# Low weight parts of three plain pairs of the MLP made by a negated copy and an adding DMA

## The chip, the cores and the metric

The kernel runs on one core of a Trainium2 chip. The metric is the device time of one execution in microseconds (us), here the median of several. The core has five engines that run beside each other and wait for each other by semaphores: TensorE (PE in the profile, with its weight loads as PEld), VectorE (DVE), ScalarE (ACT), GpSimd (POOL) and SyncE (SP). SP computes nothing here; it issues the DMA transfers that bring weights from the chip's main memory.

## The reference: two layers of a hybrid decoder

Activations are 256 x 2048 in float32, and there are two layers. A layer computes

- `proj = rms_norm(x) @ w_in`, whose columns feed eight heads of gated linear attention and eight heads of stick-breaking attention;
- `x = x + mixed @ w_o`, with the normalised outputs of both groups in `mixed`;
- `up = square(relu(rms_norm(x) @ w_up))` with 8192 columns, and `x = x + up @ w_down`.

The two matrices of the MLP (2048 x 8192 and 8192 x 2048) hold most of the weights. Each weight is used once per layer, for all 256 tokens.

## The kernel before

**Products in two parts.** TensorE multiplies at its fast rate in a rounded type, fp32r. To keep float32 accuracy the kernel splits each operand in a high part (the value rounded to fp32r) and a low part (the value minus its high part), and replaces a product by three: high by high, high by low, low by high. For a weight tile, ScalarE makes the high part `whi` with a rounding copy (L984) and VectorE the low part `wlo` with a subtraction (L988). This is `parts`.

**Units and pairs.** The listed stage of a layer (`listed`) is a list of units. A unit multiplies an operand by 1024 columns of weights. In the MLP there are four quarters q, and each holds four units: `up` with n2 = 0 and 1, then `down` with n2 = 0 and 1. Over both layers that makes 16 up units and 16 down units. A unit runs over eight pairs j = 0 to 7; a pair is two blocks of 128 rows of weights, loaded by one SP transfer of 1 MB into a tile `raw` (128 partitions x 2 rows k x 1024 columns). There are four such raw tiles. The transfer for pair x waits in SP's queue until every reader of pair x - 4 is done.

**Plain and fast pairs.** Some pairs are computed by a scheme that saves a product by sums of blocks (`FAST`: pairs 1, 2, 4, 5 of an up unit and 1, 4, 5 of a down unit); VectorE forms these sums of weights (L821) before the parts are made. A fast pair has four pieces of parts, with 2, 1, 2 and 2 products. The other pairs are plain: two pieces, one for each half of 512 columns c, each holding both rows k. A product is the three matmuls of `product` (L1078), each 128 x 128 by 512 columns. A plain piece feeds two banks of the accumulator, banks 2 and 4 for c = 0 and banks 3 and 8 for c = 1, with the products of both rows k in each, so it is 12 matmuls.

**The ring.** The parts live in a ring of five slots (`RING`). Piece i may be written only when the matmuls of piece i - 5 are done, which leaves four pieces of matmuls as its lead.

**Banks and seeds.** In a down unit each of banks 2, 4, 3 and 8 starts from the residual: ScalarE copies `xt` into it (`seeds`, L1100) before its first matmul. It can do so only when VectorE has taken the sums of the unit before out of that bank (`finals`, L821). In an up unit the first matmul clears the bank, and only the `finals` of the unit before have to be done. At the start of a unit that follows an up unit, TensorE also transposes that unit's result (L1233), after the first and after the second piece.

**Order.** `Plan` sets the order of all this. Each piece of work has an engine, a planned length and a lag. TensorE's and SP's orders are as written; a due time is worked out backwards for the others, and a simulated run gives ScalarE and VectorE, whenever one is free, the ready piece that is due first. The instructions are then written out in that order, engine by engine, and each engine runs its own list in order. In this stage GpSimd has a few memsets, in the units before the MLP.

Of the kernel before, what the change touches and what calls it, by code (L numbers as in the profile page):

```python
# [11 lines left out]
F32R = mybir.dt.float32r  # L12
BF16 = mybir.dt.bfloat16
AF = mybir.ActivationFunctionType
ALU = mybir.AluOpType
AX = mybir.AxisListType

P = 128
# [21 lines left out]
class Plan:  # L40
# [20 lines left out]
    def add(self, engine, length, fn, *deps, lag=0.0):  # L61
        flat = []
        for d in deps:
            flat.extend(d if isinstance(d, (list, tuple)) else [d])
        self.pieces.append(Plan.Piece(engine, length, fn, [d for d in flat if d], lag))
        return self.pieces[-1]

    def run(self):
        t = 0.0
        for p in self.pieces:  # L70
            if p.engine == "PE":
                p.due = t
                t += p.length
        begins = {"DVE": t, "ACT": t}
        unset = {p: len(p.users) for p in self.pieces if p.engine != "PE"}
        last = []

        def settled(p):
            for d in p.deps:
                if d in unset:  # L80
                    unset[d] -= 1
                    if not unset[d]:
                        push(d)

        def push(p):
            end = min([u.due for u in p.users], default=t) - p.lag - self.GAP
            heapq.heappush(last, (-end, -at_of[p], p))

        at_of = {p: i for i, p in enumerate(self.pieces)}
        for p in self.pieces:  # L90
            if p in unset and not p.users:
                push(p)
        for p in reversed(self.pieces):
            if p.engine == "PE":
                settled(p)
        while last:
            end, _, p = heapq.heappop(last)
            p.due = min(-end, begins.get(p.engine, t)) - p.length
            if p.engine in begins:
                begins[p.engine] = p.due  # L100
            settled(p)
        line = {e: [p for p in self.pieces if p.engine == e] for e in ("PE", "SP")}
        free = dict.fromkeys(("PE", "SP", "DVE", "ACT"), 0.0)
        left = {p: len(p.deps) for p in self.pieces}
        at = dict.fromkeys(self.pieces, 0.0)
        ready = {"DVE": [], "ACT": []}
        order, events, count = [], [], 0
        for p in self.pieces:
            if not p.deps:
                events.append((0.0, count, p))  # L110
                count += 1
        came = set()
        while events:
            now, _, p = heapq.heappop(events)
            if p is not None:
                if p.engine in ready:
                    heapq.heappush(ready[p.engine], (p.due, count, p))
                else:
                    came.add(p)
                count += 1  # L120
            for e in free:
                if free[e] > now + 1e-9:
                    continue
                if e in ready:
                    if not ready[e]:
                        continue
                    p = heapq.heappop(ready[e])[2]
                elif line[e] and line[e][0] in came:
                    p = line[e].pop(0)
                else:  # L130
                    continue
                order.append(p)
                free[e] = now + p.length
                heapq.heappush(events, (free[e], count, None))
                count += 1
                for u in p.users:
                    at[u] = max(
                        at[u], free[e] + p.lag + (0.0 if u.engine == e else self.GAP)
                    )
                    left[u] -= 1  # L140
                    if not left[u]:
                        heapq.heappush(events, (at[u], count, u))
                        count += 1
        assert len(order) == len(self.pieces)
        for p in order:
            if p.fn:
                p.fn()
        return max(free.values())
# [3 lines left out]
def trunk_kernel(  # L152
# [17 lines left out]
    nc = tc.nc  # L170
# [51 lines left out]

    ATT = ("v4", "tri", "nones", "ident16", "wg", "reset", "mask16", "lr", "lrT", "ha", "hh", "hl", "hA", "on", "row", "bc")
    MLP = (*(f"{t}{i}" for t in ("whi", "wlo") for i in range(4, 12)), "sxh1", "sxk", "sx1", "sx2", "ts", "t4", "raw2")
    MANUAL = {mybir.EngineType.SP, mybir.EngineType.PE, mybir.EngineType.DVE, mybir.EngineType.Activation}

    def tmp(tag, shape, dt=F32, bufs=2):
        pool = pools["att"] if tag in ATT else pools["mlp"] if tag in MLP else tpool
        return pool.tile(list(shape), dt, tag=tag, name=nm(tag), bufs=bufs)
# [7 lines left out]
    def f32(ap):  # L237
        return ap.bitcast(F32)
# [173 lines left out]
            return self.t[k // 2][:, k % 2].rearrange("p a t -> p (a t)")  # L412

    FAST = {"up": (1, 2, 4, 5), "down": (1, 4, 5)}
    KEPT = 4
    HEAD_KINDS = ("sk", "sv", "gv")
    QUICK = (
# [158 lines left out]
    def part_tile(tag, turn, shape):  # L576
        slot = f"{tag}{turn % 4}"
        return ppool.tile(shape, F32R, tag=slot, name=nm(tag), bufs=1)
# [229 lines left out]
    def listed(l, front, mixed=None, old=None, linear=None):  # L808
# [7 lines left out]
        add = plan.add  # L816
        MM, TR, V2, V1, A2, A1 = 0.227, 0.108, 1.15, 0.61, 1.0, 0.55
        RING, RAWS = 5, 4
# [30 lines left out]
        free = {}  # L849
        whi, wlo, raws = [], [], []  # L850
        part_base = part_turn[0] % 4
        up, done = {}, {}
# [119 lines left out]
        def parts(src, readers, deps, n=2):  # L972
# [23 lines left out]
            readers.extend((h, lo))  # L996
            return box, h, lo

        last = {}
        sums13, sums4 = [], []  # L1000


        def steps(u, j, is_fast, r, ld, readers):

            kind, q, _ = units[u]
            op = {
                "gg": hT_now, "o": mixed, "up": hm, "down": up.get(q),
                "sk": hT, "sv": hT, "gv": hT,
            }[kind]

            def blk(k, tt, j=j):
                sl = slice(tt * P, (tt + 1) * P)
                return lambda: (op.t[j][:, k, 0, sl], op.t[j][:, k, 1, sl])

            def ext(i):
                return lambda: (op.x[j][:, i, 0, :], op.x[j][:, i, 1, :])

            if isinstance(ld, dict):
                for c, ms in ((0, (2, 4)), (1, (3, 8))):
                    for k in range(2):  # L1020
                        yield parts(
                            lambda c=c, k=k: r()[:, k : k + 1, c * 512 : (c + 1) * 512],
                            readers, ld[c, k], 1,
                        ), [(m, [(blk(k, tt), 0)]) for tt, m in enumerate(ms)]
                return
            if not is_fast:
                for c, ms in ((0, (2, 4)), (1, (3, 8))):
                    yield parts(
                        lambda c=c: r()[:, :, c * 512 : (c + 1) * 512], readers, ld
                    ), [(m, [(blk(k, tt), k) for k in range(2)]) for tt, m in enumerate(ms)]  # L1030
                return
            box = {}

            def row(k):
                return r()[:, k, :].rearrange("p (c n) -> p c n", c=2)

            def b12():
                return r()[:, 0, 512:]

            def first():  # L1040
                box["13"] = tmp("ts", [P, 2, 512], bufs=1)
                ends = r().rearrange("p k (c n) -> p (k c) n", c=2)[:, ::3, :]
                combine(box["13"], ends, b12().unsqueeze(1).to_broadcast([P, 2, 512]))

            def fourth():
                box["4"] = tmp("t4", [P, 512], bufs=1)
                combine(box["4"], b12(), r()[:, 1, :512])

            t13 = add("DVE", V2, first, ld, sums13[-1] if sums13 else [])
            t2 = vector(b12, lambda: box["13"][:, 0, :], lambda: r()[:, 1, 512:], t13)  # L1050
            t4 = add("DVE", V1, fourth, t2, sums4[-1] if sums4 else [])
            readers.extend((t13, t2, t4))
            sums13.append([])
            sums4.append([])
            yield parts(lambda: row(1), readers, ld), [
                (2, [(blk(1, 0), 0)]), (3, [(ext(1), 1)]),
            ]
            yield parts(lambda: box["4"].unsqueeze(1), sums4[-1], t4, 1), [
                (4, [(blk(1, 1), 0)]),
            ]  # L1060
            yield parts(lambda: box["13"], sums13[-1], t13), [
                (5, [(ext(3) if op in (hT, hT_now) or kind == "up" and j == KEPT else blk(0, 1), 0)]), (7, [(ext(2), 1)]),
            ]
            yield parts(lambda: row(0), readers, t2), [
                (1, [(blk(0, 0), 0)]), (6, [(ext(0), 1)]),
            ]
# [849 lines left out]
```

## Time and profile before

| | |
|---|---|
| median of three runs | 2138.92 us (2138.73 to 2139.3) |
| span of the profiled execution | 2137.1 us |
| TensorE busy | 2128.5 us, 10114 matmuls, mean granted clock 0.999 |
| VectorE busy | 1930.0 us (90%) |
| ScalarE busy | 1422.7 us (67%) |
| GpSimd busy | 31.5 us, 57 instructions |
| transfers of SP's queue | 413.53 MB, 55.8% of the 16 DMA engines' span |

The profile is one execution. Its span runs from the first to the last instruction; the device time of a run has a little more around it, 1.8 us between this span and the median. No device time is given for the profiled execution itself. A busy TensorE is not by itself a TensorE at its peak, since matmuls overlap and their ends are modelled; the distance between the starts of consecutive matmuls says more. In a row of a timeline stand the start in us, the duration in us, the engine, the line, the operation, and the tiles as out<-in. Names such as `m__1106_5066` are banks in the accumulator, and the number tells one use of a bank from another.

### The profile page before, as it was taken

The numbers are of one execution on the slowest core, as the hardware profiler recorded it, in microseconds if no ns is written. First come the engines' busy times: TensorE is split into PE (matmuls) and PEld (weight loads), VectorE is DVE, ScalarE is ACT, GpSimd is POOL, SyncE is SP. The second block draws the span as 40 slices with busy tenths as digits, with TensorE's granted clock in tenths as the row PEclk, the third lists the DMA queues.
The fourth block names the chain that finished last, engine by engine and source line by source line (L and its number), as shares of the span: only waits on it lengthen the run. The fifth ranks groups of instructions, "written<-read, shape, count | busy, mean of one in ns | idle before, by whom it ended". The sixth has DMA issues, their size and how long they took to land.

```text
span 2137.1 us, 27196 instructions
## 1 busy us (share of the span) xinstructions
PE 2128.5 (100%) x10114; PEld 1776.4 (83%) x10114; DVE 1930.0 (90%) x2403; ACT 1422.7 (67%) x2101; POOL 31.5 (1%) x57
## 2 busy tenths in 40 slices
PE   9999999999999999999999999999999999999999
PEld 7888888888888888888888988888888888888887
DVE  7977689999999899899999676899999999998997
ACT  7667677666576567566666585876765665765674
POOL 0001000000000000000000010000000000000000
PEclk9999999999999999999999999999999999999999
DMA  7645545565556556555666544556555655564564
GB/s 257 215 146 174 178 177 185 198 211 184 207 196 218 177 197 217 196 193 201 217 206 208 164 155 159 198 190 221 179 210 185 216 180 214 191 223 177 197 211 144
DMA packets 131448, 415.26 MB, mean 194 GB/s; under 512 B 6794, under 2 KB 31954, under 8 KB 131316
## 3 DMA queue, kind: packets, MB, share of 16 engines
q1 hardware_dynamic: 131316, 413.53, 55.8%
q8 instruction: 79, 1.29, 0.2%
q14 instruction: 53, 0.43, 0.1%
HBM read 409.31 MB, written 4.19 MB: 193 GB/s over the span
## 4 chain that ended last, share of the span: by engine, by line
PE 97%; issue 1%; DVE 1%; ACT 1%; DMA 0%; POOL 0%; POOLq 0%
PE acc L634 2%; PE acc L609 1%; PE acc L638 1%; PE acc L612 1%; PE acc L615 1%; PE m__38_167 L1078 1%; PE m__40_173 L1078 0%; PE m__2636_12050 L1078 0%; PE m__596_2644 L1078 0%; PE m__691_3115 L1078 0%; PE m__2731_12521 L1078 0%; PE m__602_2669 L1078 0%; PE m__2642_12075 L1078 0%; PE m__50_207 L1078 0%; PE m__2641_12066 L1078 0%
## 5 line engine op out<-in xcount | busy, mean ns | idle before, releaser
L984 ACT ACTIVATE whi<-raw 128x1024 fp32r<-128x1024 f32 (+1 forms) x706 | 733.8, 1055 | 383.7 <-issue 25.4
L988 DVE TENSOR_TENSOR wlo<-raw,whi 128x1024 fp32r<-128x1024 f32 (+1 forms) x706 | 844.0, 1216 | 27.3 <-ACT whi L984 19.0
L984 ACT ACTIVATE whi<-ts 128x1024 fp32r<-128x1024 f32 x138 | 145.9, 1057 | 113.3 <-PE m__3146_14472 L1078 6.5
L988 DVE TENSOR_TENSOR wlo<-ts,whi 128x1024 fp32r<-128x1024 f32 x138 | 168.8, 1223 | 47.7 <-ACT whi L984 47.6
L821 DVE TENSOR_TENSOR ts<-raw 128x1024 f32<-128x1024 f32 x138 | 168.3, 1219 | 0.6
L593 DVE TENSOR_TENSOR wlo<-raw,whi 128x1024 fp32r<-128x1024 f32 (+2 forms) x80 | 81.3, 1017 | 38.9 <-ACT whi L592 38.2
L984 ACT ACTIVATE whi<-t 128x512 fp32r<-128x512 f32 x138 | 86.2, 625 | 41.7 <-DVE t L821 12.6
L988 DVE TENSOR_TENSOR wlo<-t,whi 128x512 fp32r<-128x512 f32 x138 | 94.6, 685 | 10.0 <-ACT whi L984 9.9
L592 ACT ACTIVATE whi<-raw 128x1024 fp32r<-128x1024 f32 (+2 forms) x80 | 71.1, 889 | 46.0 <-PE acc L615 21.6
L821 DVE TENSOR_TENSOR t<-raw 128x512 f32<-128x512 f32 x138 | 94.7, 686 | 1.2
L821 DVE TENSOR_TENSOR raw<-ts,raw 128x512 f32<-128x512 f32 x138 | 94.5, 685 | 0.4
L634 PE MATMUL acc<-act,whi 128*128 128x512 f32 x256 | 91.9, 400 | 0.0
L638 PE MATMUL acc<-act,wlo 128*128 128x256 f32 x256 | 72.0, 281 | 0.0
L1212 ACT ACTIVATE act<-act,st 128x512 f32<-128x512 f32 x64 | 44.4, 716 | 32.6 <-DVE act L821 32.6
L609 PE MATMUL acc<-whi,act 128*128 128x272 f32 (+2 forms) x192 | 62.8, 327 | 0.0
L612 PE MATMUL acc<-wlo,act 128*128 128x272 f32 (+2 forms) x192 | 61.5, 320 | 0.0
L615 PE MATMUL acc<-whi,act 128*128 128x272 f32 (+2 forms) x192 | 61.4, 320 | 0.0
L634 PEld LDWEIGHTS acc<-act,whi 128*128 128x128 f32 x256 | 48.1, 188 | 10.2
L638 PEld LDWEIGHTS acc<-act,wlo 128*128 128x128 f32 x256 | 48.4, 189 | 0.1
L492 DVE TENSOR_TENSOR act<-act,act 128x512 fp32r<-128x512 f32 x64 | 42.5, 685 | 0.0
L609 PEld LDWEIGHTS acc<-whi,act 128*128 128x128 f32 x192 | 36.4, 190 | 3.6 <-issue 0.7
L488 ACT ACTIVATE act<-act 128x512 fp32r<-128x512 f32 x64 | 39.0, 622 | 0.5
(2819 smaller groups left out, 5771.6 us busy)
## 6 DMA issues: line engine op xcount, KB each, us to landing
raw<-in_w_up_dram SPq DMA_DIRECT2D x128, 1024.0 KB, 4.9
raw<-in_w_down_dram SPq DMA_DIRECT2D x128, 1024.0 KB, 5.4
raw<-in_w_in_dram SPq DMA_DIRECT2D x87, 1024.0 KB, 5.4
raw<-in_w_o_dram SPq DMA_DIRECT2D x32, 1024.0 KB, 5.1
raw<-in_w_in_dram SPq DMA_DIRECT2D x8, 544.0 KB, 3.8
raw<-in_w_in_dram SPq DMA_DIRECT2D x8, 512.0 KB, 3.7
act<-in_x_dram SPq DMA_DIRECT2D x7, 512.0 KB, 8.0
xs<-act SPq DMA_DIRECT2D x4, 512.0 KB, 3.0
```

Source lines behind the costliest of these rows:

```text
L492: nc.vector.tensor_tensor(lo, src, f32(h), ALU.subtract)
L592: newest["hi"] = nc.scalar.activation(hi[:, :, :width], r, AF.Copy).ins
L593: newest["lo"] = nc.vector.tensor_tensor(lo[:, :, :width], r, f32(hi[:, :, :width]), ALU.subtract).ins
L609: nc.tensor.matmul(o, xh[:, sl], whi[:, j, :width], start=(k == 0), stop=False)
L612: nc.tensor.matmul(o, xh[:, sl], wlo[:, j, :width], start=False, stop=False)
L615: nc.tensor.matmul(o, xl[:, sl], whi[:, j, :width], start=False, stop=(k == KT - 1))
L634: nc.tensor.matmul(acc[f], whi[:, j, sl], op.both(k), start=(k == 0), stop=False, skip_group_check=True,)
L638: nc.tensor.matmul(acc[f][:, T:], wlo[:, j, sl], xh, start=False, stop=(k == KT - 1), skip_group_check=True,)
L821: nc.vector.tensor_tensor(dst, a, b, op)
L984: nc.scalar.activation(box["h"][:, :n], src(), AF.Copy)
L988: nc.vector.tensor_tensor(box["l"][:, :n], src(), f32(box["h"][:, :n]), ALU.subtract)
L1212: nc.scalar.activation(box[h][:, tt, :], box[h][:, tt, :], AF.Relu, scale=rr[:, tt : tt + 1],)
```

## The change

Pair 0 of each up unit and pairs 0 and 3 of each down unit, all of them plain, are split another way. Their two pieces are the rows k = 0 and k = 1 with all 1024 columns, so that a piece is one contiguous row of 4 KB on each partition. For each piece ScalarE makes the high part as before and a second copy with scale -1, the negated high part, in the place of the low part. Then a DMA issued by GpSimd adds the raw row to it, which gives raw minus high. VectorE has no part in it. A piece then feeds four banks (2, 4, 3, 8) with one product each, 12 matmuls as before. The raw tile is read by the DMA too, so it comes free when the DMA has landed. GpSimd's order is now written out by the plan as well: its pieces are taken in the order written, like SP's.

```diff
-        line = {e: [p for p in self.pieces if p.engine == e] for e in ("PE", "SP")}
-        free = dict.fromkeys(("PE", "SP", "DVE", "ACT"), 0.0)
+        line = {e: [p for p in self.pieces if p.engine == e] for e in ("PE", "SP", "POOL")}
+        free = dict.fromkeys(("PE", "SP", "POOL", "DVE", "ACT"), 0.0)
...
-    MANUAL = {mybir.EngineType.SP, mybir.EngineType.PE, mybir.EngineType.DVE, mybir.EngineType.Activation}
+    MANUAL = {mybir.EngineType.SP, mybir.EngineType.PE, mybir.EngineType.DVE, mybir.EngineType.Activation, mybir.EngineType.Pool}
...
+    ADDED = {"up": (0,), "down": (0, 3)}
...
+        def added_parts(src, readers, deps):
...
+            def high():
+                box["h"] = part("whi")
+                nc.scalar.activation(flat(box["h"]), src(), AF.Copy)
+
+            def minus():
+                box["l"] = part("wlo")
+                nc.scalar.activation(flat(box["l"]), src(), AF.Copy, scale=-1.0)
+
+            def low():
+                nc.gpsimd.dma_start(f32(flat(box["l"])), src(), accum_op=ALU.add)
+
+            h = add("ACT", A2, high, deps, whi[i - RING])
+            m = add("ACT", A2, minus, deps, wlo[i - RING])
+            lo = add("POOL", 1.2, low, m, lag=4.0)
+            whi.append([])
+            wlo.append([])
+            readers.extend((h, lo))
+            return box, h, lo
...
+            if not is_fast and j in ADDED.get(kind, ()):
+                for k in range(2):
+                    yield added_parts(lambda k=k: r()[:, k, :], readers, ld), [
+                        (m, [(blk(k, tt), c)])
+                        for c, ms in ((0, (2, 4)), (1, (3, 8))) for tt, m in enumerate(ms)
+                    ]
+                return
```

More of the change, by code (lines that the diff above doesn't have):

```diff
@@ L997, in parts, with part, flat @@
             return box, h, lo
+        def added_parts(src, readers, deps):
+            box = {}
+            i = len(whi)
+            def part(tag):
+                if i % RING < RING - 4:
+                    return tmp(f"{tag}{4 + i % RING}", [P, 2, 512], F32R, bufs=1)
+                return part_tile(tag, i % RING - (RING - 4) + part_base, [P, 2, 512])
+            def flat(t):
+                return t.rearrange("p c n -> p (c n)")
+            def high():
[13 more added lines that the diff above has]
+            return box, h, lo
         last = {}
```

## The prediction

> **What bounds the kernel now.** I read the profile's page first, then who TensorE waited for, then TensorE's timeline.
>
> ```profile
> span 2137.1 us, 27196 instructions
> ...
> PE 2128.5 (100%) x10114; PEld 1776.4 (83%) x10114; DVE 1930.0 (90%) x2403; ACT 1422.7 (67%) x2101; POOL 31.5 (1%) x57
> ...
> q1 hardware_dynamic: 131316, 413.53, 55.8%
> ...
> PE 97%; issue 1%; DVE 1%; ACT 1%; DMA 0%; POOL 0%; POOLq 0%
> ```
>
> ```profile
> PE ps L561 <- POOL ident masks.py:199: 1.5, 1, 1.5
> PE m__38_167 L1078 <- ACT whi L984: 1.4, 1, 1.4
> PE ps L699 <- DVE act L664: 1.3, 2, 0.7
> PE m__38_167 L1078 <- DVE wlo L988: 0.5, 1, 0.5
> ```
>
> TensorE is idle for 2137.1 - 2128.5 = 8.6 us, and it is 97% of the chain of waits. All its named waits, in the second fence (us in total, times, longest), come to 4.7 us; 1.8 of them are on VectorE, and none stands in an MLP unit: `m__38` is a bank of the first stage, L561 and L699 lie in the set-up and the attention. A busy TensorE could still be a slow one, so I looked at the starts of matmuls where a down unit follows a down unit (start, duration):
>
> ```profile
> 525.41 0.39 PE L1078 MATMUL m__1027_4701<-whi,act 128*128 128x512 f32 x1
> 525.64 0.39 PE L1078 MATMUL m__1100_5033<-whi,act 128*128 128x512 f32 x1
> ...
> 527.00 0.39 PE L1078 MATMUL m__1102_5051<-whi,act 128*128 128x512 f32 x1
> ...
> 529.72 0.39 PE L1078 MATMUL m__1106_5066<-whi,act 128*128 128x512 f32 x1
> ```
>
> From 525.64 to 529.72 lie the 18 matmuls of banks 2, 4 and 3, so one takes 4.08 / 18 = 0.2267 us, and the unit's last matmul and the next unit's first are 0.23 apart: no seam at all. The MLP runs at TensorE's own pace. VectorE, though 90% busy, ends no wait there.
>
> **The change, part by part.** The durations are those of these groups (last columns: busy us, mean ns of one):
>
> ```profile
> L984 ACT ACTIVATE whi<-raw 128x1024 fp32r<-128x1024 f32 (+1 forms) x706 | 733.8, 1055 | 383.7 <-issue 25.4
> L988 DVE TENSOR_TENSOR wlo<-raw,whi 128x1024 fp32r<-128x1024 f32 (+1 forms) x706 | 844.0, 1216 | 27.3 <-ACT whi L984 19.0
> ```
>
> *Removed.* 16 up units x 1 pair + 16 down units x 2 pairs = 48 pairs, 96 pieces: 96 x 1.216 = 117 us of VectorE, which would go from 90% to about 85%. On the path: nothing, since it ends no wait of TensorE's in these units.
>
> *Added on ScalarE.* 96 negated copies, taken at the 1.055 us of the high copy (same size, same engine): 101 us, 67% to 71%. Beside other work; the cover is ScalarE's idle time, by stretch:
>
> ```profile
> 482.30:525.60 43.30, 43.30 (x200) 36.01 (x200) 42.10 (x50) 29.41 (x39) 0.00 (x0) 1.00 0.58 203
> 525.60:568.50 42.90, 42.90 (x191) 35.51 (x191) 37.48 (x41) 24.25 (x27) 0.00 (x0) 1.00 0.56 196
> ```
>
> These are the two down units of one quarter (columns: length, then busy PE, PEld, DVE, ACT, POOL, clock, DMA share, GB/s). Four more copies make ScalarE 33.6 of 43.3 and 28.5 of 42.9. Copies that came in a crowd would delay the pieces behind them in ScalarE's order, which is the lateness priced below.
>
> *TensorE's work.* The same 24 matmuls per pair, the same shapes: 0. Their order moves, and with it when a bank is needed. Bank 8's first matmul was the 19th of the unit and becomes the 10th, bank 3's was the 13th and becomes the 7th. The cover was the long wait of these banks; what is left of it in the two kinds of down units:
>
> ```profile
> 482.34 0.39 PE L1078 MATMUL m__1019_4664<-whi,act 128*128 128x512 f32 x1
> ...
> 483.81 0.58 ACT L1100 ACTIVATE m__1027_4701<-act 128x512 f32<-128x512 f32 x1
> ```
>
> ```profile
> 526.12 1.05 ACT L984 ACTIVATE whi<-ts 128x1024 fp32r<-128x1024 f32 x1
> 527.07 0.58 ACT L1100 ACTIVATE m__1106_5066<-act 128x512 f32<-128x512 f32 x1
> ```
>
> Needed now at 482.34 + 9 x 0.2267 = 484.38 and 525.64 + 2.04 = 527.68; the seeds as they stand end at 484.39 and 527.65. In the second kind that is from 529.72 - 527.65 = 2.1 us of slack to none. Taking 0.1 us from a seed's end to the matmul (half of the 0.2 us quoted below for a start after a release), each kind is late by about 0.1: 16 x 0.1 = 1.6 us. From below 0: due times are worked out anew, and the first seed waits behind other work, as the second does behind a `whi` copy of 1.05. From above one VectorE or ScalarE instruction in the way, half of 1.1 on average: 16 x 0.55 = 9 us. Bank 3 stays clear:
>
> ```profile
> 482.35 0.58 ACT L1100 ACTIVATE m__1024_4688<-act 128x512 f32<-128x512 f32 x1
> ```
>
> ```profile
> 525.58 0.60 ACT L1100 ACTIVATE m__1104_5055<-act 128x512 f32<-128x512 f32 x1
> ```
>
> Its seeds end at 482.93 and 526.18, its new times are 6 matmuls (1.36) after the unit's first, 483.70 and 527.00: 0. The up units need no seed, which saves them that step of 0.6 us: 0.
>
> *Added on GpSimd and the DMA engines.* 96 adding transfers of 512 KB. Nothing in this trace shows one. The wait is in GpSimd's queue, for the negated copy; behind it stand only the next adding transfers (POOL has x0 in the windows above), and for those waits TensorE. The nearest rows (last column: us from issue to landing):
>
> ```profile
> raw<-in_w_up_dram SPq DMA_DIRECT2D x128, 1024.0 KB, 4.9
> raw<-in_w_down_dram SPq DMA_DIRECT2D x128, 1024.0 KB, 5.4
> ...
> raw<-in_w_in_dram SPq DMA_DIRECT2D x8, 512.0 KB, 3.7
> ...
> xs<-act SPq DMA_DIRECT2D x4, 512.0 KB, 3.0
> act<-xs SPq DMA_DIRECT2D x4, 512.0 KB, 7.6
> ```
>
> ```profile
> 494.03 0.37 SPq L934 DMA_DIRECT2D raw<-in_w_down_dram  x1
> ```
>
> ```profile
> L1834 POOL TENSOR_TENSOR act<-act,row 128x512 f32<-128x512 f32 (+1 forms) x12 | 17.2, 1461 | 80.2 <-ACT act L1829 80.2
> ```
>
> Landing lies between 3.0 (512 KB out of on-chip memory) and 7.6 (512 KB queued among others). An add must fetch both addends, 1 MB in all, so I take the rows that move 1 MB, 5.2 between 4.9 and 5.4. The issue lies between SP's 0.37 and GpSimd's 1.46 of an ordinary instruction; I take the middle, 0.9. So 6.1 us from the end of the negated copy, ends 3.4 and 9.1.
>
> What it may take follows from the ring. The tightest is the first piece of pair 3 in a down unit: its slot comes free after the single product of fast pair 1's second piece, and four pieces of 6, 6, 12 and 12 matmuls follow.
>
> ```profile
> 491.41 0.39 PE L1078 MATMUL m__1021_4676<-whi,act 128*128 128x512 f32 x1
> ...
> 499.80 0.39 PE L1078 MATMUL m__1019_4664<-whi,act 128*128 128x512 f32 x1
> 500.03 0.39 PE L1078 MATMUL m__1019_4664<-wlo,act 128*128 128x512 f32 x1
> ```
>
> ```profile
> 491.55 2.95 ACT L984 ACTIVATE whi<-raw 128x1024 fp32r<-128x1024 f32 x3
> ```
>
> ```profile
> 476.90 0.39 PE L1078 MATMUL m__934_4298<-whi,act 128*128 128x512 f32 x1
> ```
>
> ```profile
> 477.10 1.06 ACT L984 ACTIVATE whi<-raw 128x1024 fp32r<-128x1024 f32 x1 [1.66 <-PE m__948_4350 L1078]
> ```
>
> The last two show that ScalarE starts 0.2 us after the piece before is done. The slot is free at 491.64 + 0.2 = 491.84, and the low part is first read at 500.03. In this unit ScalarE is in a group of three copies from 491.55; if the negated copy goes second it ends near 493.6 and leaves 6.4 us. In the other kind of down unit ScalarE has more room: 500.03 - 491.84 - 1.06 = 7.1. Against 6.1 both hold, by 0.3 and 1.0 us. The second piece has 1.36 us more lead; pair 0, with four plain pieces ahead (48 x 0.2267 = 10.9), over 2 more. Cost 0, and thin.
>
> *SP's queue.* The raw tile now comes free when its DMA has landed. SP waits almost only for raw tiles to come free:
>
> ```profile
> SPq L934 <- DVE wlo L988: 1488.8, 315, 10.4
> ```
>
> The refill behind pair 3 would issue near 493.6 + 1.36 + 6.1 = 501.1 and, by 5.4, land at 506.5. Pair 7, which it serves, starts on TensorE at 499.8 + 2 x 5.44 (two plain pairs of 24 matmuls) + 2 x 4.76 (two fast ones of 21) = 520.2, and its first slot is free four pieces (12, 12, 6 and 6 matmuls, 8.2 us) before that, at 512.0: 0, with 5.5 us to spare.
>
> *DMA engines.* SP's 413.53 MB took 55.8% of 2137.1 us, 347 GB/s. The 50 MB more take 145 us by what is written, 290 by what is read: 55.8% to 63 or 69%. That shows in the profile, and delays only what is late already.
>
> **Sum.** 0 + 0 + 1.6 + 0 + 0 = +1.6 us: the span from 2137.1 to 2138.7, and by the same 1.8 us between span and median, 2140.5 us.
>
> **Rivals.** *(1) The adding transfers of pair 3 land late: slower.* Place: TensorE, at `wlo` of pair 3 in each of the 16 down units. It decides from 6.4 us after the negated copy in one kind and 7.1 in the other. For it: my 6.1 is a guess between far ends, two such transfers follow each other, and SP issues a load of 1 MB at 494.03, in their midst. Against it: the 512 KB rows at 3.0 and 3.7. At 7.6 it costs 8 x 1.2 + 8 x 0.5 = 13.6 us on top of the seeds, 2154; at the upper end of 9.1, 8 x 2.7 + 8 x 2.0 = 38, 2178.
>
> *(2) Bank 8's seed is in the way.* The upper price above, +9: 2148. For it: the needed time has no slack left in either kind. Against: VectorE is relieved just ahead of it.
>
> *(3) GpSimd cannot issue while VectorE works.* If an issue had to wait for the VectorE instruction under way, 1.2 us at the longest, 6.1 becomes 7.3: 8 x 0.9 + 8 x 0.2 = 9, about 2149; if it waited for a real gap, VectorE being busy for 42.1 of 43.3 us, tens of microseconds, 2170 and more. Nothing in this trace shows GpSimd issuing a transfer, for or against.
> [...]
>
> *(4) VectorE's relief reaches TensorE: faster.* At most VectorE's 1.8 us of named waits, which lie outside the changed units; to pass the bound of 0.2% half of all idle time would have to go. 2137 at best, or a little under.
>
> **How the numbers follow.** The measurement tells about 0.2%, 4.3 us, from no change. The forecast holds with 0.48, rival 1 with 0.28, rival 2 with 0.12, rival 3 with 0.07, rival 4 with 0.05 (nearly all of it still under 4.3 us, so I give faster 0.04). Slower is 1 to 3 together, 0.47; same is the rest, 0.49. The forecast's own range is 2137 to 2143. To leave out no more than two in ten, the range reaches to 2160: that holds rival 2 and the nearer two thirds of rival 1, and leaves out its far end and most of rival 3.
>
> **What would show it.** Right: TensorE's busy time within 3 us of before and matmul starts 0.227 apart in pair 3 of a down unit; VectorE near 1815 us, ScalarE near 1524; the DMA share between 0.63 and 0.69; adding transfers that land some 5 us after issue, ahead of their first matmul. Wrong: a wait of TensorE's at L1078 for a DMA, about a microsecond long and 16 or 32 times (rival 1); for ScalarE at the 10th matmul of a down unit (rival 2); long gaps on GpSimd between the negated copy's end and the transfer's start that end with VectorE's instructions (rival 3). A median over 2143.2 proves the forecast wrong, whichever it is.

## The result, and the profile after

The changed kernel takes 2221.27 us (median of four, 2217.22 to 2226.41) against 2138.84: ratio 1.0386, 95% interval 1.0369 to 1.0404. It is 82 us slower, 61 us above the end of the predicted range. The page of the profiled execution, which took 2217.22 us:

```profile
span 2215.5 us, 27597 instructions
...
PE 2156.7 (97%) x10114; PEld 1782.4 (80%) x10114; DVE 1843.9 (83%) x2307; ACT 1513.1 (68%) x2197; POOL 114.4 (5%) x153
...
q1 hardware_dynamic: 131316, 413.53, 54.9%
q0 software_dynamic: 13824, 50.34, 12.2%
...
PE 65%; DMA 18%; issue 8%; DVE 4%; ACT 4%; POOL 0%; SPq 0%; POOLq 0%; ACTq 0%
...
raw<-in_w_down_dram SPq DMA_DIRECT2D x128, 1024.0 KB, 5.9
wlo<-raw POOLq DMA_DIRECT2D x96, 512.0 KB, 9.0
```

TensorE now has 2215.5 - 2156.7 = 58.8 us of idle time where it had 8.6, and transfers are 18% of the chain of waits where they were 0% (11% the adding ones, the rest loads). An adding transfer takes 9.0 us from issue to landing (4.5 to 11.5 over the 96), and this time counts from the start of GpSimd's issue. Who TensorE waited for (four rows of the list; us in total, times, longest):

```profile
PE m__1332_6091 L1118 <- DMA wlo<-raw: 4.2, 2, 3.2
PE m__3766_17356 L1118 <- DMA wlo<-raw: 4.1, 2, 3.3
...
PE m__1020_4667 L1118 <- DMA wlo<-raw: 3.0, 2, 1.7
...
PE m__2816_13019 L1118 <- ACT m__2816_13019 L1140: 0.2, 1, 0.2
```

Every wait of over 1.7 us in total is for `wlo`; the seed of a bank (last row) is worth 0.2 us and is listed three times in all. Pair 3 of the same down unit that the prediction worked on, on TensorE's timeline:

```profile
493.31 0.39 PE L1118 MATMUL m__1045_4784<-whi,act 128*128 128x512 f32 x1
...
501.47 0.39 PE L1118 MATMUL m__1020_4667<-whi,act 128*128 128x512 f32 x1
503.52 0.50 PE L1118 MATMUL m__1020_4667<-wlo,act 128*128 128x512 f32 x1 [1.66 <-DMA wlo<-raw]
...
506.14 0.39 PE L1118 MATMUL m__1020_4667<-whi,act 128*128 128x512 f32 x1
507.85 0.50 PE L1118 MATMUL m__1020_4667<-wlo,act 128*128 128x512 f32 x1 [1.31 <-DMA wlo<-raw]
```

The slot of its first piece is free when the next piece's first matmul starts, at 493.31, and TensorE is there 8.16 us later, the 36 matmuls that the prediction counted. Both of the pair's low parts are late, by 1.82 and 1.48 us beyond the usual 0.23. What happened in between, on ScalarE, GpSimd and SP:

```profile
494.33 1.06 ACT L985 ACTIVATE whi<-raw 128x1024 fp32r<-128x1024 f32 x1
495.28 2.00 ACT L1019 ACTIVATE wlo<-raw 128x1024 fp32r<-128x1024 f32 x2
```

```profile
496.63 1.80 POOL L1022 DMA_DIRECT2D wlo<-raw  x2 [17.60 <-ACT wlo L1019]
```

```profile
497.40 0.37 SPq L935 DMA_DIRECT2D raw<-in_w_down_dram  x1
```

The two negated copies go at 495.28, the first adding transfer at 496.63 and the second 0.95 us behind it, at 497.58 (the row merges the two); between them SP issues the load of pair 6.

**A wait here costs more than its length.** At nine of its waits in this execution TensorE got half its clock for 3.41 us. One of them (timeline, then two windows with busy PE, PEld, DVE, ACT, POOL, clock, DMA share, GB/s):

```profile
684.79 0.80 PE L1118 MATMUL m__1332_6091<-wlo,act 128*128 128x512 f32 x1 [3.17 <-DMA wlo<-raw]
...
685.81 0.63 PE L1118 MATMUL m__1336_6114<-whi,act 128*128 128x512 f32 x1
686.24 0.63 PE L1118 MATMUL m__1336_6114<-wlo,act 128*128 128x512 f32 x1
```

```profile
680.91:684.32 3.41, 0.72 (x4) 0.24 (x2) 2.09 (x3) 1.06 (x1) 0.00 (x0) 1.00 0.51 102
684.32:687.73 3.41, 2.94 (x7) 2.36 (x8) 0.78 (x2) 0.00 (x0) 0.00 (x0) 0.50 0.49 130
```

Matmuls start 0.43 us apart instead of 0.227. The granted clock is 0.50 for a stretch of 3.41 us, which begins while TensorE still waits, 2.7 us into the wait. The trace's clock records hold nine such stretches at waits, and the mean clock is 0.992 (0.999 before). All nine start whole multiples of 3.413 us apart, within 0.01 us, so their starts lie on one grid. In the 3.413 us ahead of each, one window of that grid, TensorE was idle for 1.86 to 3.28 us by its records (2.69 in the stretch shown); the windows behind which the clock stayed full were idle for 1.85 us at most. What sets the clock, no run here shows. Some 59 matmuls beyond the 7 of before were paced that way, which is 59 x 0.2 = 12 us.

So of the 78 us that the span grew, 50 are idle time of TensorE and about 12 the half clock; the rest lies in matmul records that the waits stretched and in small gaps, and was not taken apart further.

### The profile page after: what moved, and what is told of

It reads as the page before. It is cut to its first block, busy times and chain, and to the rows that moved or that the text cites. A ratio compares the mean times of both kernels' runs of the same rounds, so it can differ in the third digit from the quotient of the medians.

```text
span 2215.5 us, 27597 instructions
## 1 busy us (share of the span) xinstructions
PE 2156.7 (97%) x10114; PEld 1782.4 (80%) x10114; DVE 1843.9 (83%) x2307; ACT 1513.1 (68%) x2197; POOL 114.4 (5%) x153
## 3 DMA queue, kind: packets, MB, share of 16 engines
q1 hardware_dynamic: 131316, 413.53, 54.9%
q0 software_dynamic: 13824, 50.34, 12.2%
## 4 chain that ended last, share of the span: by engine, by line
PE 65%; DMA 18%; issue 8%; DVE 4%; ACT 4%; POOL 0%; SPq 0%; POOLq 0%; ACTq 0%
DMA wlo<-raw 11%; DMA raw<-in_w_down_dram 6%; DVE wlo L989 2%; PE acc L635 2%; ACT whi L985 1%; PE acc L610 1%; PE acc L639 1%; PE acc L613 1%; PE acc L616 1%; DMA raw<-in_w_up_dram 1%; PE m__38_167 L1118 1%; ACT wlo L1019 0%; PE m__40_173 L1118 0%; PE m__2636_12098 L1118 0%; PE m__596_2644 L1118 0%
## 5 line engine op out<-in xcount | busy, mean ns | idle before, releaser
L985 ACT ACTIVATE whi<-raw 128x1024 fp32r<-128x1024 f32 (+1 forms) x610 | 635.0, 1055 | 387.2 <-issue 32.1
L989 DVE TENSOR_TENSOR wlo<-raw,whi 128x1024 fp32r<-128x1024 f32 (+1 forms) x610 | 731.7, 1217 | 154.0 <-ACT whi L985 145.2
L1022 POOL DMA_DIRECT2D wlo<-raw x96 | 82.9, 863 | 1577.1 <-DVE wlo L989 611.9
L1015 ACT ACTIVATE whi<-raw 128x1024 fp32r<-128x1024 f32 x96 | 100.3, 1053 | 22.5 <-PE m__776_3565 L1118 1.7
L1019 ACT ACTIVATE wlo<-raw 128x1024 fp32r<-128x1024 f32 x96 | 99.8, 1048 | 0.0
L635 PEld LDWEIGHTS acc<-act,whi 128*128 128x128 f32 x256 | 48.1, 188 | 10.2
```

Of the source, the lines that this page charges most:

```text
L635: nc.tensor.matmul(acc[f], whi[:, j, sl], op.both(k), start=(k == 0), stop=False, skip_group_check=True,)
L985: nc.scalar.activation(box["h"][:, :n], src(), AF.Copy)
L989: nc.vector.tensor_tensor(box["l"][:, :n], src(), f32(box["h"][:, :n]), ALU.subtract)
L1015: nc.scalar.activation(flat(box["h"]), src(), AF.Copy)
L1019: nc.scalar.activation(flat(box["l"]), src(), AF.Copy, scale=-1.0)
L1022: nc.gpsimd.dma_start(f32(flat(box["l"])), src(), accum_op=ALU.add)
```

## The experiments

Three theories were put to the test. A: the adding transfers land after the first matmul that reads them, above all in pair 3 (A1: because they stand behind SP's loads; A2: for some other reason of their own). B: the new order of the banks costs the time. C: GpSimd cannot issue while VectorE works.

**Pair 3 alone, and pair 0 alone.**

```diff
-    ADDED = {"up": (0,), "down": (0, 3)}
+    ADDED = {"down": (3,)}
```

> Only pair 3 of the down units is changed. Theory A (the adding transfers land after their first matmul, mostly in pair 3): in the profile of the changed kernel some 48 us of TensorE's waits and most of the half-speed clock windows lie at pair 3, so about 60 us of the 82 stay: near 2200 us, with some ten half-speed windows. Theory B (the cost comes from the new order of banks, needed earlier at the start of a unit): pair 0 is as before, so the time falls back to that of before, within 4 us. Theory C (GpSimd cannot issue while VectorE works): 32 of 96 transfers are left, so a third of the cost, some 27 us: 2166.

```diff
-    ADDED = {"up": (0,), "down": (0, 3)}
+    ADDED = {"up": (0,), "down": (0,)}
```

> Only pair 0 of the up and the down units is changed. Theory A: pair 0 has 10.9 us of lead against some 9 us from issue to landing and a negated copy of 1 us, so few waits stay, those of the second down unit and of some up units, 6 to 9 us of waits and seeds: 2145 to 2150. Theory B: nearly all of the cost stays: 2210 to 2221. Theory C: two thirds stay: 2193.

Measured: pair 3 alone 2201.64 us, ratio 1.0293 (1.0278 to 1.0308); pair 0 alone 2160.39, ratio 1.0102 (1.0087 to 1.0117). The excesses, 63 and 21 us, add up to 84, about the 82 of the whole. Pair 3 carries three quarters with a third of the transfers, as A has it; B and C expected the reverse order. Pair 0 costs about twice the most that I had expected (11 us). Its longest waits are short:

```profile
PE m__3766_17330 L1118 <- DMA wlo<-raw: 1.1, 1, 1.1
PE m__3454_15910 L1118 <- DMA wlo<-raw: 1.0, 2, 0.7
```

Here too a transfer lands in 9.0 us at the median and in 10.7 at most. It is mostly issued 8.4 to 10.3 us ahead of the first matmul that reads it, so pair 0's lead of 10.9 us is just spent. By the starts of matmuls the late low parts take 12 of the 21 us; where the rest lies was not followed up.

**The rows without the transfer.** All three pairs split by rows, with VectorE's subtraction:

```diff
-            def minus():
-                box["l"] = part("wlo")
-                nc.scalar.activation(flat(box["l"]), src(), AF.Copy, scale=-1.0)
-
             def low():
-                nc.gpsimd.dma_start(f32(flat(box["l"])), src(), accum_op=ALU.add)
+                box["l"] = part("wlo")
+                combine(flat(box["l"]), src(), f32(flat(box["h"])), ALU.subtract)
...
-            m = add("ACT", A2, minus, deps, wlo[i - RING])
-            lo = add("POOL", 1.2, low, m, lag=4.0)
-            whi.append([])
+            lo = add("DVE", V2, low, h, wlo[i - RING])
+            whi.append([lo])
```

> All three pairs are split by rows and feed the four banks as in the changed kernel, but VectorE subtracts the high part again; no negated copy and no adding transfer. Theory A: only bank 8's seed is left, 0 to 5 us: 2139 to 2144. Theory B: the cost stays, above 2200. Theory C: as theory A.

Measured: 2140.64 us, ratio 1.0008 (0.9999 to 1.0017). The new order of the banks costs 1.7 us against its own runs of before; the interval reaches from -0.2 to +3.6, so it is not told apart from 0. Theory B falls. The seed's wait is there, once, in this kernel's list:

```profile
PE m__2040_9299 L1114 <- ACT m__2040_9299 L1136: 0.2, 1, 0.2
```

**A copy in place of the add.** This kernel leaves the addition out and keeps the rest; its low part is then the whole weight, which changes the values but neither the number nor the sizes of its instructions.

```diff
-                nc.gpsimd.dma_start(f32(flat(box["l"])), src(), accum_op=ALU.add)
+                nc.gpsimd.dma_start(f32(flat(box["l"])), src())
```

> The changed kernel with plain transfers in place of the adding ones: the raw row is copied over the negated part, so the low part holds the weight itself and the addition is left out. Theory A with the add's own price: an adding transfer keeps the 16 engines 2.7 us, twice a raw load per byte; copied it should take 1.3 us, the first piece land near 5 and the second near 6.5 us after issue instead of 6 and 10, and TensorE's waits fall from some 55 us to under 15: 2145 to 2165. Theory C: GpSimd issues as many transfers and writes as much, so the cost stays: above 2200. If the loads ahead in the queue are all that matters, landing falls by under 2 us and the time lies near 2190.

Measured: 2160.07 us, ratio 1.0099 (1.0082 to 1.0115). Rows of the page, of the changed kernel and then of this one (the page's groups, its DMA queues, its DMA issues):

```profile
L1022 POOL DMA_DIRECT2D wlo<-raw x96 | 82.9, 863 | 1577.1 <-DVE wlo L989 611.9
```

```profile
q0 software_dynamic: 13824, 50.34, 5.9%
...
L1022 POOL DMA_DIRECT2D wlo<-raw x96 | 50.9, 530 | 1555.2 <-DVE wlo L989 599.1
...
wlo<-raw POOLq DMA_DIRECT2D x96, 512.0 KB, 6.8
```

The same bytes as a copy take 5.9% of the 16 engines' span, as an add 12.2%. That is 2.8 us of all 16 engines for one adding transfer (0.122 x 2215.5 / 96) against 1.3 for a copy. GpSimd's issue takes 0.33 us less and the transfer lands 2.2 us sooner, and 61 of the 82 us are gone, as A with the add's own price expected. Theory C, by which as many issues should cost as much, falls with it. The changed kernel shows it directly. A transfer was issued at 541.40 while VectorE was busy throughout, and from 542.8 it filled the engines (window of 1.43 us from the issue, columns as above; then the queues from 542.8 to 544.3; a share comes out above 100% where packets overlap):

```profile
541.40:542.83 1.43, 1.43 (x8) 1.20 (x7) 1.43 (x2) 1.43 (x2) 0.86 (x1) 1.00 0.24 95
```

```profile
q0 software_dynamic: 79, 0.32, 116.6%
```

And of the changed kernel's 96 issues 95 begin within 0.33 us of the end of their negated copy and none takes over 1.02 us, though the page's row puts much of GpSimd's idle time down to VectorE.

**Behind which loads?** In the changed kernel SP issues two loads, and GpSimd an adding transfer right after:

```profile
428.55 0.37 SPq L935 DMA_DIRECT2D raw<-in_w_up_dram  x1
```

```profile
430.82 0.37 SPq L935 DMA_DIRECT2D raw<-in_w_up_dram  x1
```

```profile
430.99 0.86 POOL L1022 DMA_DIRECT2D wlo<-raw  x1 [39.49 <-DVE wlo L989]
```

The queues from 431.5 to 435.5, and from 437.5 to 440.5 (packets, MB, share of the 16 engines):

```profile
q1 hardware_dynamic: 309, 1.20, 100.5%
```

```profile
q0 software_dynamic: 165, 0.61, 103.2%
q1 hardware_dynamic: 11, 0.03, 3.0%
```

For 4 us the engines serve SP's queue alone, though GpSimd's transfer was issued 0.5 us before; its first bytes move at 436.11, 5.1 us after its issue. The one issued at 541.40, with the engines at a share of 0.24 up to 542.83, started in 1.4 us. From 437.5 to 440.5 the engines serve GpSimd's queue nearly alone. To see whether that order is what makes pair 3 late, I held back the load between its two transfers. First by telling the plan (`adding` lists the pieces of the adding transfers):

```diff
...
-            piece = add("SP", 2.9, fn, raws[x - RAWS] if x >= RAWS else [], lag=4.6)
+            late = adding[-2:] if units[u][0] == "down" and i == 6 else []
+            piece = add("SP", 2.9, fn, raws[x - RAWS] if x >= RAWS else [], late, lag=4.6)
...
```

> The changed kernel, and SP's load for pair 6 of each down unit waits until both adding transfers of pair 3 have landed, so that no load comes between the two. Theory A1 (the 16 engines serve transfers of both queues in order of issue, so that an adding transfer waits for every load issued before it): the second transfer of pair 3 lands some 2.5 us sooner, near 7.5 us after its issue, and most of the waits of over 2.4 us go, with the half-speed windows behind them: 40 to 50 us of the 82 come back, 2170 to 2180. Rival A2 (the queues share the engines, and the second transfer is late because it follows the first, or because GpSimd is slow): it still lands 9 to 10 us after issue, and the time stays above 2205. If the held loads come too late themselves, TensorE waits behind pair 6's parts and the time is above 2221.

Measured: 2216.19 us, ratio 1.0358 (1.0339 to 1.0376). The landing is 9.0 us as before. This edit held nothing: a dependence of the plan only shapes the planned order, SP's order is fixed anyway, and the instruction still waits for its data alone. In its trace SP still issues that load less than 1.6 us ahead of pair 3's second transfer in 14 of the 16 down units. It tells nothing of A1 or A2. Beside it ran the plan's lag:

```diff
-            lo = add("POOL", 1.2, low, m, lag=4.0)
+            lo = add("POOL", 1.2, low, m, lag=8.5)
```

> The changed kernel with the plan's lag of an adding transfer at 8.5 us in place of 4.0, so that the plan knows how late it lands and puts the negated copies earlier in ScalarE's order. Theory A: in the first down unit of a quarter the negated copies of pair 3 start some 2 us after their slot is free; they can gain up to that, in 8 of 16 units, for about 15 us with the clock: 2200 to 2210. If the plan's order was the cause rather than the transfer, nearly all of the 82 us come back: under 2150. If the earlier copies push other work out, 2221 or more.

> Both edits together, the held load of pair 6 and the lag of 8.5 us. Theory A: their gains add where they concern different units, 2155 to 2170; pair 0's 21 us stay in any case, so not under 2150. If the two concern the same waits, as the held load alone.

Measured: 2198.9 (1.0281, 1.0261 to 1.0301) and with the ineffective hold 2197.76 (1.0275, 1.0259 to 1.0291), the same within their intervals. The plan's wrong lag is worth some 22 us, a little more than A expected; the rest it cannot mend. The same first piece in the run with the lag alone, GpSimd's issue and TensorE's first two matmuls:

```profile
495.64 0.85 POOL L1022 DMA_DIRECT2D wlo<-raw  x1 [16.66 <-DVE act L493]
```

```profile
502.15 0.39 PE L1118 MATMUL m__1020_4667<-whi,act 128*128 128x512 f32 x1
502.38 0.39 PE L1118 MATMUL m__1020_4667<-wlo,act 128*128 128x512 f32 x1
```

Its slot is free at 493.76, by the start of the next piece's first matmul, and the issue follows after 1.88 us where it took 3.3; the wait is gone. The earlier issue is ScalarE's order, as A expected. But the landing also fell, from 6.8 to 4.9 us, and SP's load now comes 3.4 us behind the issue instead of 0.8.

Then with a real hold: SP copies 256 bytes of the second low part to a small tensor `mark` in main memory, and stands until that low part has landed (`adding` now keeps the piece and its tiles).

```diff
...
+            if units[u][0] == "down" and i == 6:
+                lo, low = adding[-1]
+                add("SP", 0.1, lambda: nc.sync.dma_start(mark, f32(low["l"])[0:1, 0, 0:64]), lo)
             readers = []
             piece = add("SP", 2.9, fn, raws[x - RAWS] if x >= RAWS else [], lag=4.6)
...
```

> In the run before this one the plan was told of the held load, but the instructions never waited for it: SP's loads went out as in the changed kernel. Here SP first copies 256 bytes of the second low part of pair 3 to memory, which can go only when the adding transfer has landed, and pair 6's load stands behind it in SP's queue. Theory A1 (the 16 engines take transfers about in order of issue): the second adding transfer starts right behind the first, lands near 7.5 us after its issue instead of 10, and 30 to 45 us of the 82 come back: 2175 to 2190. Rival A2 (the load between the two is not what holds the second): it still lands 9 to 10 us after issue: above 2210. If pair 6's load is late instead, waits appear behind pair 6's parts and the time is above 2221 with the second transfer early.

> The real hold and the plan's lag of 8.5 us together; the lag alone gave 2199. Theory A1: its gain of 20 us lies in the first down unit of a quarter, the hold's mostly in the second, so 2155 to 2175. Rival A2: 2195 to 2205.

Measured: 2153.25 us, ratio 1.0067 (1.0052 to 1.0082); with the lag of 8.5, 2160.82, ratio 1.0099 (1.0082 to 1.0116). The hold gives back 68 of the 82 us, more than I had expected. A1 expected the lag's gain to come on top of it; instead the lag costs 7.6 us here, and why was not followed up. Pair 3's first matmuls in the held kernel, at the place shown above:

```profile
500.65 0.39 PE L1123 MATMUL m__1020_4667<-whi,act 128*128 128x512 f32 x1
500.88 0.39 PE L1123 MATMUL m__1020_4667<-wlo,act 128*128 128x512 f32 x1
...
503.40 0.39 PE L1123 MATMUL m__1020_4667<-whi,act 128*128 128x512 f32 x1
503.63 0.39 PE L1123 MATMUL m__1020_4667<-wlo,act 128*128 128x512 f32 x1
```

No wait at either piece; the seam is 0.23 us. The first was issued at 495.80, as late after its slot as in the changed kernel (free at 492.49, 3.3 us), and it landed in 4.9 us. And SP did wait at the new line, 16 times:

```profile
SPq L940 <- DMA wlo<-raw: 206.2, 16, 14.0
```

That is A1. The second transfer of pair 3 lands in 6.2 us at the median of the 16 down units, where it took 10.2 in the changed kernel; pair 0's transfers, whose loads nobody held, still take 9.2. So the median of all 96 falls only to 8.3:

```profile
wlo<-raw POOLq DMA_DIRECT2D x96, 512.0 KB, 8.3
```

None of pair 3's 32 low parts is waited for any more. Last, pair 3 alone with the real hold (the two edits above together):

> Pair 3 of the down units alone, with the real hold of pair 6's load; without the hold it gave 2202. Theory A1: with no load between, both adding transfers of pair 3 land within some 7 us and the first matmuls do not wait; pair 0 is as before the change, so the time is that of before within 0.2%: 2137 to 2143. If an adding transfer itself were too long for pair 3's lead, 16 to 32 waits of half a microsecond or more stay: 2147 and up. Faster than before is not expected, since TensorE has no waits on VectorE there to give back.

Measured: 2139.74 us, ratio 1.0001 (0.9992 to 1.0010). Its page:

```profile
span 2138.1 us, 27340 instructions
...
PE 2129.4 (100%) x10114; PEld 1776.2 (83%) x10114; DVE 1897.6 (89%) x2371; ACT 1450.5 (68%) x2133; POOL 59.1 (3%) x89
...
wlo<-raw POOLq DMA_DIRECT2D x32, 512.0 KB, 5.4
```

The same row with pair 3 alone and no hold:

```profile
wlo<-raw POOLq DMA_DIRECT2D x32, 512.0 KB, 9.6
```

Landing falls from 9.6 us to 5.4, and none of the 32 transfers takes over 6.8. Held, they cost nothing; the relief of VectorE by 32 subtractions brings nothing either. No version ran faster than the kernel before.

## Why the prediction was wrong

- **What bounds the kernel: right.** TensorE had no time to gain. Pair 3's share of the work, taken off VectorE without late parts (pair 3 held), moves the time by 0.01%, within an interval of -0.08% to +0.10%: rival 4 falls, as far as these 32 of the 96 pieces go.
- **Removed work and copies: right in kind.** The two groups in the changed kernel:

```profile
L989 DVE TENSOR_TENSOR wlo<-raw,whi 128x1024 fp32r<-128x1024 f32 (+1 forms) x610 | 731.7, 1217 | 154.0 <-ACT whi L985 145.2
...
L1019 ACT ACTIVATE wlo<-raw 128x1024 fp32r<-128x1024 f32 x96 | 99.8, 1048 | 0.0
```

  VectorE's group of raw subtractions fell from 844.0 to 731.7 us, and a negated copy took 1.048 us against the 1.055 taken. VectorE's busy time fell only to 1843.9, not to 1815. The durations of its instructions do fall by 115 us in all; but they overlap a little where they follow each other closely (145 us in all before, 117 after), and busy time counts an overlap once.
- **Banks and seeds: the slack was right, the price by luck.** +1.6 us predicted, 1.7 measured for the row order by itself. But the trace of that run doesn't show 0.1 us in each of 16 units. One matmul starts 0.37 us late behind its seed, and seven more follow a seed that ended 0.05 us before them, with starts 0.24 to 0.25 us apart: some 0.5 us in all. Rival 2 falls.
- **The adding transfer: the step that failed.** I took 6.1 us from the negated copy to the landing, with ends 3.4 and 9.1. It lands in 9.0 at the median and 11.5 at most, counted from the issue. Where no load comes between (pair 3 held), my price was not bad: issue 0.86 us against 0.9, and 5.4 for issue and landing together against 6.1. (The rows I took 5.2 us from count from the issue already, so I had counted an issue twice.) What I left out of the sum is the queue. The row that showed it was in my fence: 512 KB in 7.6 us "queued among others". I kept it as a far end and took the rows of 1 MB instead, although I had noted SP's load at 494.03 in the midst of the pair. Here the loads go out in bursts (100.5% of the engines' time from 431.5 to 435.5), and what stands ahead is part of the price, not its bad luck. The add's double engine time, 2.8 us against a copy's 1.3, is the second part; I had guessed at it by two addends, but what the engines fetch for an add no run shows. In sum, a load (1 MB at 413.53 MB per 54.9% of 2215.5 us: 3.1 us) and two adds (2.8 us each) are 8.7 us of engine time. In the unit shown, the second low part would have been read at 501.47 + 13 x 0.227 = 504.42 without any wait, 7.8 us after the first issue: too early for all three, whatever their start costs. Without the load, 5.6 us of engine time fit. Each of the two parts alone gives most of the time back (68 us by the hold, 61 by the copy): the lateness took both.
- **The lead: right to the hundredth, its use wrong.** 8.16 us are there. But I let the negated copy go second in its group, from a free slot at 491.84 to its end near 493.6; in the run the transfer issued 496.63 - 493.31 = 3.3 us after the slot came free, because the plan, which believed in 1.2 + 4.0 us, put other work first. With the lag of 8.5 the issue came 1.88 us after the slot, and this unit's first piece no longer waited. This is the smaller part: in the held kernel the issue was as late as before and nothing waited.
- **Rival 1: the right mechanism at a fifth to six tenths of its price.** I gave it 0.28 and 14 to 38 us; pair 3 alone costs 63. The second transfers land in 10.2 us at the median, beyond my far end. Beside that, I had counted one lateness per unit where both pieces can be late, and nothing for the half clock behind waits.
- **Pair 0: the lead was right, the cost of 0 wrong.** With issues mostly 8.4 to 10.3 us ahead of need and a landing of 9.0, nothing is left of 10.9 us, and it costs 21 us alone. The held kernel still pays 14. All its waits for low parts stand at pair 0 (9 us by the starts of matmuls); that the other 5 lie there too is a difference, since pair 3 held costs nothing.
- **SP's queue: 0, as far as the lists show.** SP waits for adding transfers at 47 loads (520.8 us in all). VectorE waits 2.4 us in all for loads of `w_down`, and no wait of TensorE's is listed for a load.
- **DMA engines: right and no comfort.** 54.9 + 12.2 = 67% lies within the 63 to 69% I gave, and the line "delays only what is late already" was the error above in short form: a mean share says nothing of a burst (67% over the span, 100.5% from 431.5 to 435.5).
- **Rival 3: refuted.** A transfer began 1.4 us after its issue with VectorE busy throughout. VectorE ran TENSOR_TENSOR instructions beside all 96 issues, beside 35 of them without a gap; how an issue fares beside its other instructions, no run here shows. The chance of 0.07 was an estimate of mine with no row behind it.

The measured time lies outside the range because the range was built on the rivals' prices, and the likeliest rival's price stopped at 9.1 us for one late piece per unit.

## What to carry to other kernels

A transfer that has to arrive in time is priced with what stands ahead of it in the engines (here the hold of one load per down unit gave back 68 of 82 us): look at the timeline of the other queue's issues, not at the mean share, and add the engine time of what was issued before it (here 3.1 us for each load of 1 MB) to the time that it takes alone. Where its lead is tight, keep the other queue's loads from slipping in between by a wait that the hardware sees; a dependence in a planner is not one. And where the bounding engine has no wait on the engine you relieve, as here, the relief itself is worth nothing (0.01% for 32 subtractions), so every new latency is pure risk.

## What I had not expected of the hardware

- The two queues hardly shared the engines in these stretches: of the engines' time, SP's queue had 100.5% from 431.5 to 435.5 and GpSimd's none; from 437.5 to 440.5 it was 3.0% and 103.2%. In the pair shown, whose transfers went out at 496.63 (add), 497.40 (load) and 497.58 (add), GpSimd's had 111.2% from 498.3 to 500.3 and SP's none, then SP's 103.0% against 0.2% from 502.3 to 503.7, then GpSimd's 101.2% against 4.2% from 504.8 to 506.5: about the order of issue. Two loads issued up to 2.4 us before GpSimd's transfer kept its first bytes back for 5.1 us after its issue, where 1.4 us was enough at 541.40. Why they go in this order, no run here shows.
- An adding transfer took 2.1 times the engine time of a copy of the same bytes (12.2% against 5.9%, in spans of 2215.5 and 2159.4 us).
- At a wait of 3.2 us the clock fell to half for 3.41 us, and so it did behind 1.86 us of idle time that fell into one window of the 3.413 us grid.
